# A hybrid decoder layer on one core: gates moved ahead of pooling, top-k rounds tile by tile, and small work taken off VectorE

## The chip, the cores and the metric

One Trainium2 chip, of which the kernel uses one core. The core has a matrix engine (TensorE, PE in the profile, with its weight loads as PEld), a vector engine (VectorE, DVE), a scalar engine (ScalarE, ACT), GpSimd (POOL) and SyncE (SP), which issues DMAs. Each engine runs its own queue in order and waits on semaphores. The metric is the device time of one execution in microseconds (us), the median of several runs.

## What is computed

One layer over x of 512 tokens by 1024 channels, in float32. One input projection feeds three token mixers; each mixer's output is gated, projected to 1024 channels, and the three are merged with sigmoid gates:

```python
u = x @ w_in + b_in                      # split into 19 pieces
y_a = pool_mixer(a_x) * silu(a_z)        # trailing means over 2, 4, 8, 16 tokens, per channel group
y_b = dsa_mixer(...) * silu(b_z)         # 8 heads, keys chosen per query: top 128 of an indexer's score
y_c = nsa_mixer(...) * silu(c_z)         # 8 heads in 2 groups: compressed, selected and window branches
g = sigmoid(g_merge).reshape(B, S, 3, D)
m = g[:,:,0] * (y_a @ w_pa) + g[:,:,1] * (y_b @ w_pb) + g[:,:,2] * (y_c @ w_pc)
return layernorm(alpha * x + m @ w_o)
```

The pooling mixer is `mean over the last w tokens - x`, where the first w-1 tokens divide by their position. The indexer's score is a sum over 8 heads of `relu(iq . ik) * iw`. The compressed branch has 31 blocks of 32 tokens, made by a small two-layer network.

## The kernel before

**Layout.** Activations lie with channels on the 128 partitions and the 512 tokens along the row. Each float32 operand is split into a rounded high part and a rest (`split`), and each product is three matmuls (`mm3`, lines L68 to L70). A "dense" tile is one 128-channel slice of the input projection: 8 slices of x times 3 matmuls of 128x512, 24 in all, written to a PSUM tile `d` (three buffers, shared with the pooling matmul). Its weights come by `load_w`: a DMA, the high part on ACT (L93), the rest on POOL (`w_l`, L95) in the middle of the program.

**Units.** Attention is done in units of four heads by 128 queries: for the third mixer ("c") two head groups g, token tiles j = 3, 2, 1, 0, and two branches each; then for the second mixer ("b") two groups with j = 0 to 3. A unit's front computes scores (`qkc`, `qkb`, L441, four PSUM buffers), masks them and takes the row maximum on DVE (L443), exponentiates on ACT (L448), scales (ACT L460, DVE L462 into `pc` or `pb`) and transposes by a DMA on SP; its back multiplies with the values (`acc`, L479) two half-units later. The compressed branch rides on the units of branch 0: class `Compressed` takes scores of 32 blocks, their least value after scaling by -0.125, softmax and gain (L505 to L521), and its matmuls are L529. The units of the first group end with a flag `"c0"`, those of the second with `"c1"`; later work that needs them waits in the list for the flag.

**Order.** The order of PE is written by hand. One list `F` of generators holds all other matmul work: dense tiles for queries, keys, SiLU gates (`f_zc`, `f_zb`), pooling (`pool_x`, `pool_z`, `pool_y`), merge gates (`merge_g`: a dense tile, then a tanh on ACT into `tg`) and merges (`merge`: projection `pp` of a mixer's output, times the gate). Between pieces of a unit the list is advanced by fixed steps (3.25 after each half front, 2 after a front, 0.3 per piece of the back). When the list stands at a flag that is not set, it gives nothing. The order on the other engines is set by a scheduler from the program.

**Top-k.** For token tiles 1, 2, 3 of the indexer the score `acc` (128 x 256, 384, 512) is turned into a mask by 16 rounds of `topk_round`: MAX8 (L305) finds the eight largest of each row, MATCH_REPLACE8 (L306) marks them. `tk(n)` issues n rounds from a list after each front, and the second mixer's unit j needs the mask of tile j.

**Pooling.** `pool_x` adds shifted rows on POOL (L566), and on DVE corrects the first columns through a small tile `pe` (L570, L571), forms mean minus x (L572), and copies the corrected columns back (L573). `pool_y` multiplies with 128x128 weights and reads the result on DVE (L588).

**Compressed values.** `compress_v` splits the block values into three bfloat16 parts and writes each into `VC` through a block mask (`bmask`, six multiplications, L396).

Of the kernel before, what the change touches and what calls it, by code (L numbers as in the profile page):

```python
# [7 lines left out]
F32 = mybir.dt.float32  # L8
# [4 lines left out]
OP = mybir.AluOpType  # L13
# [14 lines left out]
NTILES = I_G + 24  # L28
SMALL = (("posk", 32), ("posv", 32), ("pool_b", 4), ("pool_scale", 4), ("bmask", 4), ("rcnt", 16), ("rowv", 1),
         ("mcmp", 128), ("ident", 128))  # L30
# [4 lines left out]
def trunk(ctx, tc, a, out, dbg=None):  # L35
# [345 lines left out]
    def compress_v():  # L381
        HH, HL, w2h, w2l = CP["v"] + W2[1]
        bmask = small["bmask"]
        v32 = sp.tile([128, 2, 64], F32, name="vc32", bufs=1)
        ps = dps("vc")[:, :128].rearrange("p (g d) -> p g d", g=2)
        for g in range(2):
            mm3(ps[:, g], HH[:, g].rearrange("p r n -> p (r n)"), HL[:, g].rearrange("p r n -> p (r n)"),
                w2h, w2l, True, True)
        nc.vector.tensor_scalar(v32, ps, vscale, 0.5, op0=OP.mult, op1=OP.mult)
        for p in range(3):  # L390
            v1 = sp.tile([128, 2, 64], BF, name="vc1", bufs=2)
            nc.vector.tensor_copy(v1, v32)
            if p < 2:
                nc.vector.tensor_sub(v32, v32, v1)
            for g in range(2):
                nc.vector.tensor_mul(VC[p][:, g], v1[:, g, None, :].to_broadcast([128, 4, 64]),  # L396
                                     bmask[:, :, None].to_broadcast([128, 4, 64]))
        yield
# [85 lines left out]
    class Compressed:  # L484
# [5 lines left out]
        def begin(self, j, Q, K):  # L490
# [4 lines left out]
            if j == NT - 1:  # L495
# [12 lines left out]
        def probs(self):  # L508
            g, j, s = self.g, self.j, self.s
            den, r = sm("cden", 4, 2), sm("cr", 4, 2)  # L510
            nc.vector.tensor_sub(s, s, self.mx[:, :4, None].to_broadcast([128, 4, 32]))
            nc.scalar.activation(s, s, AF.Exp, scale=self.scale)
            nc.vector.tensor_reduce(den, s, AX.X, OP.add)
# [42 lines left out]
    def pool_x(g):  # L556
# [13 lines left out]
        nc.vector.tensor_mul(e[:, :w - 1], cur[:, :w - 1], PL["rcnt"][:, :w - 1])  # L570
        nc.vector.tensor_sub(e[:, :w - 1], e[:, :w - 1], x0[:, :w - 1])  # L571
        nc.vector.scalar_tensor_tensor(x0, cur, 1.0 / w, x0, op0=OP.mult, op1=OP.subtract)  # L572
        nc.vector.tensor_copy(x0[:, :w - 1], e[:, :w - 1])  # L573
        ph = PL["x", g] = big("t", "ph", F32R)
# [21 lines left out]

    def gate_d(d, br):
        i = I_G + 3 * d + br
        ps, b = yield from dense(i)
        t = big("b", "tg", F32, (128, 512))  # L600
        with tc.high_priority():
            nc.scalar.activation(t, ps, AF.Tanh, scale=0.5, bias=bhalf[:, i:i + 1])
        return t
# [14 lines left out]
    def merge_g(br, d):  # L618
        tg[br, d] = yield from gate_d(d, br)

    def merge(br, d):
        if d + 1 < KT:
            yield from merge_g(br, d + 1)
# [107 lines left out]
    F = Stream([(compress_in, I_KC, "k"), (vscales,), (compress_in, I_VC, "v"), (f_zc, 0, 0), (compress_mid, "k"),  # L731
                (f_zc, 0, 1), (compress_k,), (compress_mid, "v"), (f_qc, 1, 0), (f_qc, 1, 1), (f_pool,), (compress_v,),
                (pool_x, 0), (pool_x, 1), (pool_z, 0), (pool_z, 1), (f_kk, 1), (pool_y, 0), (f_zc, 1, 0), (pool_y, 1),
                (pool_x, 2), (pool_x, 3), (f_zc, 1, 1), (pool_z, 3), (pool_z, 2), (pool_y, 2), (f_qb, 0, 0), (pool_y, 3),
                (merge_g, 0, 0), "c0", (f_qb, 0, 1)] + [(merge, 0, d) for d in range(4)] +
               [(f_zb, 0, 0), (f_zb, 0, 1)] + [(merge, 0, d) for d in range(4, 7)] +
               [(merge_g, 2, 0), (merge, 0, 7), "c1", (f_qb, 1, 0), (f_qb, 1, 1), (f_zb, 1, 0), (f_zb, 1, 1)] +
               [(merge, 2, d) for d in range(KT)])
    ix = Stream([(index_scores, j) for j in (1, 2, 3)])
    while ix.step():  # L740
        F.step(2)
    rounds = [(topk_round, j) for _ in range(16) for j in (1, 2, 3)] + [(topk_end, j) for j in (1, 2, 3)]
# [44 lines left out]
    for w in work:  # L787
# [12 lines left out]
        else:  # L800
# [3 lines left out]
            if j:  # L804
                tk(100)
            un = Unit(f"b{g}{j}", psum_acc(), j, qb[g], KB[0], cmask[:, 384:] if j == 0 else negm[j],
                      0, None)
        for u in range(un.nsub):
            for _ in un.front(u):
                F.step(3.25)  # L810
            with tc.issue_after(un.last.ins):
                tk(2.3)
            nsub += 1
# [97 lines left out]
def layout(v):  # L911
# [70 lines left out]
```

## Time and profile before

| | us |
|---|---|
| runs (three) | 550.96, 550.22, 551.14; median 550.96 |
| profiled execution | 547.52 |
| its span, first to last instruction | 545.7 |
| TensorE busy in it | 519.2 |
| VectorE busy | 381.6 |
| ScalarE busy | 278.7 |
| GpSimd busy | 217.8 |

Busy time is the time in which an engine had an instruction in work; for PE it does not say at which clock. The profile also gives the granted TensorE clock (1.00 is full speed), and for each wait the engine and line that ended it. In tables of groups the form is: line, engine, operation, tile written and tiles read, shape and count, then busy us and mean ns of one.

### The profile page before, as it was taken

What the parts mean: (1) busy time and instruction counts of PE and PEld (TensorE: products, weight loads), DVE (VectorE), ACT (ScalarE), POOL (GpSimd) and SP (SyncE); (2) the same over time, 40 slices, a digit from 0 to 9 for tenths busy, and PEclk for the clock granted to TensorE, in tenths of its full rate; (3) what the DMA queues carried; (4) which work ended last, traced back from release to release, by engine and by line L of the source; (5) the groups of instructions that cost most, each with busy time, mean ns of one, the idle gap of its engine ahead of it and who ended that gap; (6) DMA issues with size and microseconds to landing.
All of it is one profiled execution on the core that took longest, in us unless ns stands there. A gap on an engine that the chain in (4) does not pass through costs nothing.

```text
span 545.7 us, 7778 instructions
## 1 busy us (share of the span) xinstructions
PE 519.2 (95%) x2718; PEld 420.2 (77%) x2718; DVE 381.6 (70%) x928; ACT 278.7 (51%) x561; POOL 217.8 (40%) x190
## 2 busy tenths in 40 slices
PE   7999989989999876999999999999999999999993
PEld 4899878868778654877778877787878888887883
DVE  5774898999999999888766466666441544545366
ACT  6783466655565475546566585765632333442000
POOL 0325433465557441134544355355564211316043
PEclk8999999989999997899999999999999999999997
DMA  7622331436545243365544445545553336454012
GB/s 271 261 77 78 115 117 59 121 79 154 95 114 126 64 116 82 84 165 129 154 102 114 123 130 132 126 117 127 139 140 96 117 111 207 164 185 144 1 60 94
DMA packets 82135, 66.72 MB, mean 122 GB/s; under 512 B 67184, under 2 KB 68656, under 8 KB 82096
## 3 DMA queue, kind: packets, MB, share of 16 engines
q1 hardware_dynamic: 74912, 40.54, 27.8%
q0 software_dynamic: 7184, 25.69, 15.4%
q8 instruction: 21, 0.34, 0.3%
q14 instruction: 18, 0.15, 0.1%
HBM read 47.87 MB, written 2.10 MB: 92 GB/s over the span
## 4 chain that ended last, share of the span: by engine, by line
PE 56%; DVE 9%; DMA 2%; ACT 1%; issue 1%; DVEq 0%; ACTq 0%
PE d L68 10%; PE d L70 10%; PE d L69 10%; PE pp L68 4%; PE pp L70 4%; PE pp L69 4%; PE acc L479 3%; PE wo L70 2%; PE wo L68 2%; PE wo L69 2%; PE qkb L441 2%; PE qkc L441 2%; DMA wo_st<-in_wo_dram 1%; DVE acc L306 1%; DVE m L305 1%
## 5 line engine op out<-in xcount | busy, mean ns | idle before, releaser
L68 PE MATMUL d<-xh,w_h 128*128 128x512 f32 (+1 forms) x424 | 168.6, 398 | 5.6 <-DVE za L588 2.8
L70 PE MATMUL d<-xh,w_l 128*128 128x512 f32 (+1 forms) x424 | 166.2, 392 | 0.0
L69 PE MATMUL d<-xl,w_h 128*128 128x512 f32 (+1 forms) x424 | 166.0, 392 | 0.0
L95 POOL TENSOR_TENSOR w_l<-w_st,w_h 128x1024 fp32r<-128x1024 f32 x41 | 99.8, 2436 | 130.1 <-ACT w_h L93 129.2
L68 PEld LDWEIGHTS d<-xh,w_h 128*128 128x128 f32 x424 | 80.5, 190 | 23.7 <-DVE za L588 3.3
L70 PEld LDWEIGHTS d<-xh,w_l 128*128 128x128 f32 x424 | 80.4, 190 | 17.5 <-DVE w_l L95 0.4
L69 PEld LDWEIGHTS d<-xl,w_h 128*128 128x128 f32 x424 | 80.5, 190 | 14.0
L93 ACT ACTIVATE w_h<-w_st 128x1024 fp32r<-128x1024 f32 x53 | 56.1, 1059 | 52.0 <-DMA w_st<-in_wt_dram 23.4
L448 ACT ACTIVATE qkc<-qkc,nb 128x512 f32<-128x512 f32 (+3 forms) x64 | 32.1, 502 | 44.3 <-DVE nb L443 28.6
L632 POOL TENSOR_TENSOR m<-m,tg 128x512 f32<-128x512 f32 x16 | 21.7, 1355 | 56.2 <-DVE tg L614 54.5
L95 POOL TENSOR_TENSOR wp_l<-wp_st,wp_h 128x512 fp32r<-128x512 f32 x16 | 20.5, 1281 | 53.9 <-ACT wp_h L93 53.9
L462 DVE SCALAR_TENSOR_TENSOR pc<-qkc,r,pc 128x512 f16<-128x512 f32 (+3 forms) x64 | 32.6, 543 | 8.6 <-ACT pc L460 8.3
L460 ACT ACTIVATE pc<-qkc,r 128x512 f16<-128x512 f32 (+3 forms) x64 | 29.6, 525 | 12.7 <-issue 5.5
L443 DVE CUSTOM_DVE_ANT_0 qkc<-qkc,cmask 128x512 f32<-128x512 f32 (+3 forms) x64 | 31.3, 490 | 4.4 <-PE qkc L441 4.0
L95 DVE TENSOR_TENSOR w_l<-w_st,w_h 128x1024 fp32r<-128x1024 f32 x12 | 15.6, 1306 | 19.4 <-ACT w_h L93 19.4
L448 ACT ACTIVATE qkb<-qkb,nb 128x128 f32<-128x128 f32 (+3 forms) x32 | 16.0, 500 | 23.3 <-DVE nb L443 23.0
L92 POOL DMA_DIRECT2D w_st<-in_wt_dram x41 | 23.3, 568 | 10.2 <-POOL w_l L95 6.8
L70 PE MATMUL wo<-woh,ml 128*128 128x512 f32 (+1 forms) x72 | 26.4, 367 | 0.3 <-DVE ml L65 0.3
L69 PE MATMUL wo<-wol,mh 128*128 128x512 f32 (+1 forms) x72 | 26.3, 366 | 0.0
L68 PE MATMUL wo<-woh,mh 128*128 128x512 f32 (+1 forms) x72 | 26.3, 365 | 0.0
L306 DVE MATCH_REPLACE8 acc<-m,acc 128x256 f32<-128x256 f32 (+2 forms) x48 | 25.7, 540 | 0.0
L479 PEld LDWEIGHTS <-vh 128*64 128x64 f16 x240 | 13.8, 110 | 15.1 <-issue 15.1
(245 smaller groups left out, 1031.7 us busy)
## 6 DMA issues: line engine op xcount, KB each, us to landing
w_st<-in_wt_dram POOLq DMA_DIRECT2D x41, 512.0 KB, 3.7
w_st<-in_wt_dram SPq DMA_DIRECT2D x12, 512.0 KB, 4.6
wp_st<-in_wp_dram POOLq DMA_DIRECT2D x16, 256.0 KB, 3.0
wo_st<-in_wo_dram SPq DMA_DIRECT2D x8, 512.0 KB, 3.5
xst<-in_xT_dram SPq DMA_DIRECT2D x8, 256.0 KB, 5.1
wp_st<-in_wp_dram SPq DMA_DIRECT2D x8, 256.0 KB, 2.6
z<-in_x_dram SPq DMA_DIRECT2D x4, 512.0 KB, 4.9
wvst<-in_wve_dram SPq DMA_DIRECT2D x4, 320.0 KB, 6.9
```

Of the source, the lines that this page charges most:

```text
L68: nc.tensor.matmul(ps, wh, rh, start=start, stop=False)
L69: nc.tensor.matmul(ps, wh, rl, start=False, stop=False)
L70: nc.tensor.matmul(ps, wl, rh, start=False, stop=stop)
L92: (nc.gpsimd if POOL[0] else nc.sync).dma_start(st, src)
L93: nc.scalar.activation(h[:, :n], st, AF.Copy)
L95: eng.tensor_sub(l[:, :n], st, f(h[:, :n]))
L306: nc.vector.match_replace(negm[j], m8, negm[j], MARK)
L443: nc.vector.tensor_tensor_reduce(sc[i], sc[i], self.mask, -0.125, 3e38, OP.add, OP.min, nb[:, i:i + 1])
L448: nc.scalar.activation(sc[i], sc[i], AF.Exp, scale=-1.0, bias=nb[:, i:i + 1], accum_out=den[:, i:i + 1])
L460: nc.scalar.activation(p[:, 0, i], sc[i], AF.Copy, scale=r[:, i:i + 1])
L462: self.last = nc.vector.scalar_tensor_tensor(p[:, 1, i], sc[i], r[:, i:i + 1], p[:, 0, i], op0=OP.mult, op1=OP.subtract)
L479: nc.tensor.matmul(self.acc[64 * i:64 * i + 64], v[:, k, self.vs * 64:self.vs * 64 + 64], pw[:, z, i, k], start=first, stop=False, skip_gr ...
```

## The change

1. Merge gates. `early_g` computes a gate into a larger tile `eg` that is kept until its merge. The gates of branch 0 for d = 0 to 3 stand ahead of pooling and between its parts; those of branch 2 for d = 0 to 3 ahead of `"c1"`. `merge` skips a gate that is there. The first query tile of the second mixer (`f_qb 0 0`) moves behind `"c0"`.
2. Top-k: the rounds of tiles 1 and 2 come first, in turns, with their ends, and then the 16 of tile 3; 1.7 rounds are issued after each front, not 2.3, and a unit of the second mixer takes only the rounds that it needs itself (`tk_until`).
3. Pooling: the corrected first columns are written in place and the main operation covers the others, so the copy L573 goes.
4. Compressed values: `VC` is cleared at the start by POOL, and POOL copies the four 32-partition blocks of each part (twelve copies); the mask and its columns in the `small` load go.
5. Compressed probabilities: the subtraction L511 goes; the least score is the bias of the exponential, one call for each head. For token tile 3 the maximum is first multiplied by -0.125.

```diff
-            for g in range(2):
-                nc.vector.tensor_mul(VC[p][:, g], v1[:, g, None, :].to_broadcast([128, 4, 64]),
-                                     bmask[:, :, None].to_broadcast([128, 4, 64]))
+            for h in range(4):
+                r = slice(32 * h, 32 * h + 32)
+                nc.gpsimd.tensor_copy(VC[p][r, :, h], v1[r])
...
-            nc.vector.tensor_sub(s, s, self.mx[:, :4, None].to_broadcast([128, 4, 32]))
-            nc.scalar.activation(s, s, AF.Exp, scale=self.scale)
+            for h in range(4):
+                nc.scalar.activation(s[:, h], s[:, h], AF.Exp, scale=self.scale, bias=self.mx[:, h:h + 1])
...
-        nc.vector.tensor_sub(e[:, :w - 1], e[:, :w - 1], x0[:, :w - 1])
-        nc.vector.scalar_tensor_tensor(x0, cur, 1.0 / w, x0, op0=OP.mult, op1=OP.subtract)
-        nc.vector.tensor_copy(x0[:, :w - 1], e[:, :w - 1])
+        nc.vector.tensor_sub(x0[:, :w - 1], e[:, :w - 1], x0[:, :w - 1])
+        nc.vector.scalar_tensor_tensor(x0[:, w - 1:], cur[:, w - 1:], 1.0 / w, x0[:, w - 1:], ...)
...
+    def early_g(br, d):
+        if d % 2 == 0:
+            EG[br] = big("s", f"eg{br}{d}", F32)
+        tg[br, d] = yield from gate_d(d, br, EG[br][:, d % 2])
...
-                (f_zc, 0, 1), (compress_k,), (compress_mid, "v"), (f_qc, 1, 0), (f_qc, 1, 1), (f_pool,), (compress_v,),
-                (pool_x, 0), (pool_x, 1), (pool_z, 0), (pool_z, 1), (f_kk, 1), (pool_y, 0), (f_zc, 1, 0), (pool_y, 1),
-                (pool_x, 2), (pool_x, 3), (f_zc, 1, 1), (pool_z, 3), (pool_z, 2), (pool_y, 2), (f_qb, 0, 0), (pool_y, 3),
-                (merge_g, 0, 0), "c0", (f_qb, 0, 1)] + [(merge, 0, d) for d in range(4)] +
-               [(f_zb, 0, 0), (f_zb, 0, 1)] + [(merge, 0, d) for d in range(4, 7)] +
-               [(merge_g, 2, 0), (merge, 0, 7), "c1", (f_qb, 1, 0), (f_qb, 1, 1), (f_zb, 1, 0), (f_zb, 1, 1)] +
-               [(merge, 2, d) for d in range(KT)])
+                (f_zc, 0, 1), (compress_k,), (compress_mid, "v"), (f_qc, 1, 0), (f_qc, 1, 1), (compress_v,),
+                (early_g, 0, 0), (f_kk, 1), (early_g, 0, 1), (f_pool,), (f_zc, 1, 0), (pool_x, 0), (early_g, 0, 2),
+                (pool_z, 0), (pool_x, 1), (early_g, 0, 3), (pool_y, 0), (pool_z, 1), (f_zc, 1, 1), (pool_x, 2), (pool_y, 1),
+                (pool_z, 2), (pool_x, 3), (pool_y, 2), (pool_z, 3), (pool_y, 3),
+                "c0", (f_qb, 0, 0), (f_qb, 0, 1)] + [(merge, 0, d) for d in range(3)] + [(f_zb, 0, 0), (f_zb, 0, 1)] +
+               [(merge, 0, d) for d in range(3, 7)] + [(early_g, 2, 0), (merge, 0, 7)] +
+               [(early_g, 2, d) for d in range(1, 4)] +
+               ["c1", (f_qb, 1, 0), (f_qb, 1, 1), (f_zb, 1, 0), (f_zb, 1, 1)] + [(merge, 2, d) for d in range(KT)])
...
-    rounds = [(topk_round, j) for _ in range(16) for j in (1, 2, 3)] + [(topk_end, j) for j in (1, 2, 3)]
+    rounds = [(topk_round, j) for _ in range(16) for j in (1, 2)] + [(topk_end, 1), (topk_end, 2)]
+    rounds += [(topk_round, 3)] * 16 + [(topk_end, 3)]
...
-                tk(2.3)
+                tk(1.7)
```

**PE, around the first unit of the second head group** (token tile 3, two heads; `acc2` is the back of the last units of the first group, `d26` and `d30` are dense tiles of pooling with weights `w26`, `w30`, `pool` is the pooling matmul). Before:

```order
L479 MATMUL acc2_152<-ptc000_2122,vh_140 64x256
L441 MATMUL qkc130_2321<-ks1_1517,cq11_1099 128x512 x2
L441 MATMUL qkc130_2326<-ks1_1517,cq11_1099 128x512 x2
L479 LDWEIGHTS vh_140
L479 MATMUL acc2_152<-ptc001_2217,vh_140 64x256
```

In the changed kernel:

```order
L480 MATMUL acc2_155<-ptc000_2060,vh_140 64x256
L442 MATMUL qkc130_2293<-ks1_1268,cq11_1100 128x512 x2
L68 MATMUL d26_2245<-xh3_87,w26_h_2240 128x512
L69 MATMUL d26_2245<-xl3_91,w26_h_2240 128x512
L70 MATMUL d26_2245<-xh3_87,w26_l_2241 128x512
L68 MATMUL pool_2322<-ph_2118,plhl_1363 128x512
L69 MATMUL pool_2322<-ph_2118,plhl_1363 128x512
L70 MATMUL pool_2322<-ph_2118,plhl_1363 128x512
L68 MATMUL d30_2338<-xh0_84,w30_h_2333 128x512
L69 MATMUL d30_2338<-xl0_88,w30_h_2333 128x512
L70 MATMUL d30_2338<-xh0_84,w30_l_2334 128x512
L442 MATMUL qkc130_2342<-ks1_1268,cq11_1100 128x512 x2
```

Where the list `F` stood at its flag, two score tiles followed each other; now dense and pooling matmuls lie between them, since two dense tiles more stand ahead of the flag than before (three gates in, one query tile out).

**DVE, in the second half-unit of the first head group** (`qkc` score tiles, `pc` their probabilities, `vc` compressed values, `acc_553`, `acc_690`, `acc_855` the scores of tiles 1, 2 and 3). Before:

```order
L443 ISA qkc_1226,nb<-qkc_1226,cmask 128x512
L443 ISA nb 128x1
L396 TENSOR_TENSOR vc_151<-vc_1128,small 128x256 x2
L462 SCALAR_TENSOR_TENSOR pc_1159<-qkc_1088,r,pc_1159 128x512
L462 SCALAR_TENSOR_TENSOR pc_1159<-qkc_1132,r,pc_1159 128x512
L305 MAX m_1178<-acc_855 128x8
L305 MAX m_1181<-acc_553 128x8
```

In the changed kernel (`acc_556` and `acc_693` are tiles 1 and 2):

```order
L463 SCALAR_TENSOR_TENSOR pc_1162<-qkc_1089,r,pc_1162 128x512
L393 CAST vc_1128<-vc_1105 128x128
L463 SCALAR_TENSOR_TENSOR pc_1162<-qkc_1134,r,pc_1162 128x512
L305 MAX m_1183<-acc_693 128x8
L305 MAX m_1186<-acc_556 128x8
L444 ISA qkc_1219,nb<-qkc_1219,cmask 128x512
```

The probabilities of the first half-unit stand ahead of the next score mask and no longer behind the mask multiplications, and tile 3 has left the top-k rows.

**POOL, at the same place** (`w_st` to `w_l` are weight loads and splits). Before:

```order
L92 DMA w_st<-in_wt_dram 128x1024
L95 TENSOR_TENSOR w_l<-w_st,w_h 128x1024
L566 TENSOR_TENSOR xs<-x_1203 128x511
L567 COPY xs<-x_1203 128x1
L92 DMA w_st<-in_wt_dram 128x1024
```

In the changed kernel:

```order
L95 TENSOR_TENSOR w_l<-w_st,w_h 128x1024
L398 COPY vc_149<-vc_1114 32x2x64 x4
L92 DMA w_st<-in_wt_dram 128x1024
L398 COPY vc_150<-vc_1121 32x2x64 x4
L398 COPY vc_151<-vc_1128 32x2x64 x4
L95 TENSOR_TENSOR w_l<-w_st,w_h 128x1024
```

The twelve copies stand where pooling's first shifted add stood, between two weight splits.

More of the change, by code (lines that the diff above doesn't have):

```diff
@@ L28 @@
 NTILES = I_G + 24
-SMALL = (("posk", 32), ("posv", 32), ("pool_b", 4), ("pool_scale", 4), ("bmask", 4), ("rcnt", 16), ("rowv", 1),
+SMALL = (("posk", 32), ("posv", 32), ("pool_b", 4), ("pool_scale", 4), ("rcnt", 16), ("rowv", 1),
          ("mcmp", 128), ("ident", 128))
@@ L315, in trunk @@
     VC = [cp.tile([128, 2, 4, 64], BF, name=f"vc{p}") for p in range(3)]
+    for p in range(3):
+        nc.gpsimd.memset(VC[p], 0.0)
     CP = {}
@@ L382, in compress_v @@
         HH, HL, w2h, w2l = CP["v"] + W2[1]
-        bmask = small["bmask"]
         v32 = sp.tile([128, 2, 64], F32, name="vc32", bufs=1)
@@ L502, in begin @@
                 nc.vector.tensor_reduce(self.mx[:, :4], self.s, AX.X, OP.max)
+                nc.vector.tensor_scalar(self.mx[:, :4], self.mx[:, :4], -0.125, None, op0=OP.mult)
         def score(self, h, ps):
@@ L570, in pool_x @@
         nc.vector.tensor_mul(e[:, :w - 1], cur[:, :w - 1], PL["rcnt"][:, :w - 1])
-        nc.vector.tensor_sub(e[:, :w - 1], e[:, :w - 1], x0[:, :w - 1])
-        nc.vector.scalar_tensor_tensor(x0, cur, 1.0 / w, x0, op0=OP.mult, op1=OP.subtract)
-        nc.vector.tensor_copy(x0[:, :w - 1], e[:, :w - 1])
+        nc.vector.tensor_sub(x0[:, :w - 1], e[:, :w - 1], x0[:, :w - 1])
+        nc.vector.scalar_tensor_tensor(x0[:, w - 1:], cur[:, w - 1:], 1.0 / w, x0[:, w - 1:], op0=OP.mult,
+                                       op1=OP.subtract)
         ph = PL["x", g] = big("t", "ph", F32R)
@@ L595, in trunk, with gate_d @@
     M32 = []
-    def gate_d(d, br):
+    def gate_d(d, br, t=None):
         i = I_G + 3 * d + br
         ps, b = yield from dense(i)
-        t = big("b", "tg", F32, (128, 512))
+        t = big("b", "tg", F32, (128, 512)) if t is None else t
         with tc.high_priority():
@@ L619, in merge_g @@
         tg[br, d] = yield from gate_d(d, br)
+    EG = {}
+    def early_g(br, d):
+        if d % 2 == 0:
+            EG[br] = big("s", f"eg{br}{d}", F32)
+        tg[br, d] = yield from gate_d(d, br, EG[br][:, d % 2])
     def merge(br, d):
-        if d + 1 < KT:
+        if d + 1 < KT and (br, d + 1) not in tg:
             yield from merge_g(br, d + 1)
@@ L750, in tk, with tk_until @@
             fn(j)
+    def tk_until(j):
+        while (topk_end, j) in rounds:
+            fn, i = rounds.pop(0)
+            fn(i)
     work = []
@@ L804, in trunk @@
             if j:
-                tk(100)
+                tk_until(j)
             un = Unit(f"b{g}{j}", psum_acc(), j, qb[g], KB[0], cmask[:, 384:] if j == 0 else negm[j],
@@ L961, in layout @@
     r["rowv"] = (t >= 31).astype(f4)[:, None]
-    r["bmask"] = (t[:, None] // 32 == np.arange(4)[None]).astype(f4)
     r["rcnt"] = c(np.broadcast_to((1.0 / np.arange(1, 17)).astype(f4), (128, 16)))
```

## The prediction

> **What bounds the kernel now.** I read the page's totals and clock line first, then each engine's busy time by stretches, then TensorE alone around the places where it stands still, then what it waited for there.
>
> ```profile
> PE   519.2 (95%) x2718; PEld 420.2 (77%) x2718; DVE 381.6 (70%) x928; ACT 278.7 (51%) x561; POOL 217.8 (40%) x190
> PEclk8999999989999997899999999999999999999997
> ```
>
> TensorE (PE) is busy 95% of the span, so only its pauses and the slices with a digit below 9 in the clock line can be won; the sum of its matmuls is not touched. The next rows are stretches of the span: length, then busy time of PE, PEld, DVE, ACT and POOL, then granted clock.
>
> ```profile
> 94.00:124.00 30.00, 27.54 (x116) 22.06 (x115) 27.88 (x69) 18.81 (x36) 15.54 (x13) 0.94 0.38 91
> 124.00:154.00 30.00, 30.00 (x176) 24.37 (x175) 29.58 (x77) 16.88 (x32) 15.71 (x14) 1.00 0.61 132
> 154.00:184.00 30.00, 30.00 (x174) 23.97 (x173) 28.53 (x83) 14.82 (x33) 17.71 (x21) 1.00 0.48 119
> 184.00:216.00 32.00, 22.84 (x119) 16.19 (x118) 30.57 (x98) 20.31 (x57) 12.07 (x10) 0.89 0.28 73
> 216.00:400.00 184.00, 182.02 (x993) 145.30 (x994) 127.16 (x383) 110.67 (x253) 83.16 (x65) 0.98 0.50 127
> ```
>
> From 94 to 216, the units of the first head group, DVE is busy 27.88 + 29.58 + 28.53 + 30.57 = 116.6 of 122 us: it is the bound there, and PE falls behind it at both ends. From 216 to 400 DVE has 184.0 - 127.2 = 56.8 us free. PE alone, cut where it stops and where its clock changes (length, PE busy, granted clock):
>
> ```profile
> 112.60:115.50 2.90, 0.43 (x3) 1.00 0.31 75
> 116.80:120.20 3.40, 3.40 (x10) 0.51 1.07 154
> 184.40:187.30 2.90, 0.35 (x3) 1.00 0.00 0
> 188.50:191.90 3.40, 3.40 (x12) 0.50 0.18 46
> 191.90:197.20 5.30, 4.98 (x35) 1.00 0.62 170
> 197.20:200.40 3.20, 0.38 (x2) 1.00 0.30 82
> 200.40:210.20 9.80, 9.30 (x58) 1.00 0.28 80
> 210.20:212.40 2.20, 0.52 (x6) 1.00 0.15 30
> 212.40:222.70 10.30, 7.04 (x27) 0.50 0.26 59
> ```
>
> Idle time (length less busy): 2.47 + 2.55 + 0.32 + 2.82 + 0.50 + 1.68 + 3.26 = 13.6 us. Half clock: 3.40 + 3.40 + 7.04 = 13.8 us of matmuls that took twice their time, so 6.9 us lost. Together **20.5 us**, all that this stage can give. What PE waited for:
>
> ```profile
> PE qkc L441 <- DVE pc L462: 5.5, 3, 2.7
> PE d L68 <- DVE za L588: 2.8, 1, 2.8
> PE d L68 <- ACT z L153: 2.6, 1, 2.6
> ```
>
> Score tiles wait until DVE has read the last ones (L462), projections until DVE has freed the PSUM of a pooling tile (L588). The ACT wait stands beside a pooling matmul too and ends when the DVE queue has moved on. All are DVE's queue.
>
> **The change part by part.** First what leaves DVE between 94 and 216 (rows: operation, shape, count, then busy us and mean ns):
>
> ```profile
> L305 DVE MAX8 m<-acc 128x8 f32<-128x512 f32 x9 | 6.1, 674 | 0.0
> L306 DVE MATCH_REPLACE8 acc<-m,acc 128x512 f32<-128x512 f32 x9 | 6.0, 671 | 0.0
> L305 DVE MAX8 m<-acc 128x8 f32<-128x384 f32 x10 | 5.4, 544 | 0.0
> L396 DVE TENSOR_TENSOR vc<-vc,small 128x256 bf16<-128x256 bf16 x6 | 5.3, 929 | 0.0
> L511 DVE TENSOR_TENSOR cs<-cs,cmx 128x128 f32<-128x128 f32 x5 | 4.9, 985 | 0.1
> L306 DVE MATCH_REPLACE8 acc<-m,acc 128x384 f32<-128x384 f32 x9 | 4.9, 540 | 0.0
> L305 DVE MAX8 m<-acc 128x8 f32<-128x256 f32 x10 | 4.1, 409 | 0.0
> L306 DVE MATCH_REPLACE8 acc<-m,acc 128x256 f32<-128x256 f32 x9 | 3.6, 405 | 0.0
> L573 DVE COPY x<-pe 128x15 f32<-128x15 f32 x1 | 2.3, 2334 | 0.0
> L573 DVE COPY x<-pe 128x3 f32<-128x3 f32 x1 | 2.0, 1962 | 0.0
> ```
>
> Top-k before: 9 x 674 + 10 x (544 + 409) + 9 x (671 + 540 + 405) ns = 30.1 us. After, the order puts 11 MAX8 and 10 MATCH_REPLACE of tiles 1 and 2 each ahead of the second head group and none of tile 3: 11 x (544 + 409) + 10 x (540 + 405) = 19.9 us. That is 10.2 us less. The six multiplications by the block mask: 5.3 us less. The small copies of pooling: 4.3 us less. The subtraction of the least compressed score: 4.9 us less; one 128x4 multiplication in its stead costs between nothing and the 0.3 us by which I shorten this, 4.6. Then two of the four pooling groups now stand behind the first unit of the second head group in DVE's order, with these five operations each:
>
> ```profile
> L572 DVE SCALAR_TENSOR_TENSOR x<-xs,x 128x512 f32<-128x512 f32 x4 | 4.9, 1236 | 0.1
> L407 DVE SCALAR_TENSOR_TENSOR za<-za,z 128x512 f32<-128x512 f32 x4 | 3.2, 788 | 0.0
> L65 DVE TENSOR_TENSOR yal<-za,yah 128x512 fp32r<-128x512 f32 x4 | 3.1, 768 | 0.0
> L65 DVE TENSOR_TENSOR ph<-x,ph 128x512 fp32r<-128x512 f32 x4 | 3.0, 761 | 0.0
> L588 DVE SCALAR_TENSOR_TENSOR za<-pool,small,za 128x512 f32<-128x512 f32 x4 | 2.9, 734 | 0.0
> ```
>
> 2 x (1236 + 788 + 768 + 761 + 734) = 8.6 us. Sum: 10.2 + 5.3 + 4.3 + 4.6 + 8.6 = 33.0, so DVE has 116.6 - 33.0 = 83.6 us to do there. PE's work in the same 122 us is its busy 27.54 + 30.00 + 30.00 + 22.84 = 110.4 less half of the half-clock pieces before 216 (3.4), about 107 us at full clock; its order has as many matmuls between the first units of the two head groups as before, only others. DVE thus falls from being the bound to 78% of PE's time. Between 124 and 184, at 97%, PE did not idle at all, so it is the pile-up that stops it, not the share.
>
> The gates also fill the hole at the end. Before, the stream of projections ran dry at its mark "c0", and the last acc matmuls of the group and the score tiles behind them stood bare; after, projections and pooling stand between them. The wait for the transposed probabilities is covered by that.
>
> What takes DVE's place: the top-k and the two pooling groups land after 216, 10.2 + 8.6 = 18.8 us against 56.8 free. The later work reaches no wait of PE there as long as that margin holds.
>
> POOL gets twelve 32x128 copies and three clears, and per moved gate a split and a DMA issue. ACT gets a tanh per gate, and four small exponentials for one:
>
> ```profile
> 109.47 2.39 POOL L95 TENSOR_TENSOR w_l<-w_st,w_h 128x1024 fp32r<-128x1024 f32 x1 [3.54 <-ACT w_h L93]
> 109.49 3.84 DVE L396 TENSOR_TENSOR vc<-vc,small 128x256 bf16<-128x256 bf16 x2
> L567 POOL COPY xs<-xs 128x8 f32<-128x8 f32 x1 | 0.2, 192 | 0.0
> L258 POOL CAST ki<-ki 64x512 fp32r<-64x512 f32 x1 | 0.6, 609 | 20.2 <-DVE ki L156 20.2
> L512 ACT ACTIVATE cs<-cs 128x128 f32<-128x128 f32 x5 | 1.6, 317 | 2.5 <-DVE cs L511 2.5
> L602 ACT ACTIVATE tg<-d,bhalf 128x512 f32<-128x512 f32 x1 | 0.7, 700 | 0.0
> ```
>
> A 32x128 copy lies between the 128x8 one and the 64x512 cast, 0.19 and 0.61 us; I take 0.25, near the small one, so 3 us for twelve (7.3 at worst). POOL is idle 30.0 - 15.5 = 14.5 us between 94 and 124, so either end is hidden. Behind the copies in POOL's queue stand a weight split and the two casts of the second group's keys. PE reaches that weight after three more projections, 72 matmuls or 12 us at the 176 in 30 us of the row from 124 to 154; if the copies held POOL longer than that, PE would wait by what is over. The three clears stand at the program's start, where POOL then waits 20.2 us for DVE (the ki row): nothing. Three gates more are 3 x 2.39 = 7.2 us of splits, while two pooling groups' shifted adds leave POOL: no net. Each DMA rides POOL's queue with its split, whose order is kept. SP's queue keeps its order. ACT: 3 x 0.70 for the gates and at most 3 x 0.317 for each of eight compressed units, 9.7 us in all, against 122 - 70.8 = 51 us free from 94 to 216 and 73 after.
>
> The first two rows above are why DVE's short operations cost so much: at 109.5 POOL starts a 2.39 us split, DVE a two-input operation, and two that could take 0.4 each take 3.84 us. The changed kernel has fewer such operations, but those left (splits, gains, sums) still meet POOL. For that I keep 0.32 + 0.50 us, the small pauses in the PE rows, and one more of 0.7, half the surplus of a mean stall: 1.5 us.
>
> A rule weighs against the part of the gain that is clock. The Trainium skill, "TensorE: Matmul & The Clock Gate", Part 1, says the clock falls to half after an idle window of about 3.4 us. By that rule stops of 2.5 to 3.2 us would not cause it, and removing them would return idle time alone. The rows say otherwise in three cases of four: half clock begins 1.3, 1.2 and 0 us after stops of 2.47, 2.55 and 1.68 us, and from 124 to 184, where PE never stops, the clock is 1.00 (the fourth stop, 2.82 us, is not followed by it). I take the rows.
>
> Sum: 20.5 - 1.5 = **19.0 us**. The profiled execution took 547.5 us (span 545.7), so 528.5; the median of the runs, 550.96, lies 3.4 higher, which I carry over: **532.0 us**.
>
> **The rivals.** (1) Clock stays: stops vanish, half clock does not. Gain 13.6 - 1.5 = 12.1, 538.9 us. For it, the one stop of four that half clock did not follow; against it, the other three. The Trainium skill's rule above would give this case. (2) Half is left: one of the two places, the start or the end of the stage, still stops, because the new hand-over between DVE and POOL (DVE's third cast waits for POOL's first copies, POOL's next copies for DVE) holds DVE's queue, or DVE and POOL keep meeting. The end is worth 2.55 + 0.32 + 2.82 + 0.50 + 1.68 + 3.26 + 5.2 = 16.3 us, the start 2.47 + 1.70 = 4.2; half of the end left gives about 540 us. For it: 3.84 us at 109.5; against it: 23 us of room. (3) Slower: top-k of tile 3 comes too late for the fourth unit of the second mixer. Its 16 rounds cost 16 x (674 + 671) = 21.5 us of DVE in one chain; if 15 or more were still to do when that unit's scores are ready, PE would stop for longer than is won, up to 553.5 us. The order speaks against it: one round alone stands between the third unit's last operations and that mask, and DVE keeps 56.8 - 18.8 = 38 us free from 216 to 400. (4) Nothing: the projections taken earlier are missed later, between the second group's units, and PE stops there instead, 551 us. Against it: DVE's 127.2 of 184 us there.
>
> **How the numbers follow.** Forecast 0.70, rival (1) 0.06, (2) 0.14, (3) 0.05, (4) 0.05. The range goes from 528, where all 20.5 us come and most of the 3.4 us between profiled execution and median does not, to 541, taking in (1) and (2). Faster by over 0.2% (1.1 us, about what a measurement of this kernel can tell): 0.70 + 0.06 + 0.14 = 0.90; (4) splits into 0.03 within and 0.02 slower; with (3) slower is 0.07.
>
> **What would show it.** Right: PE without a pause over 1 us from 94 to 231, its clock 1.00 throughout, DVE near 80% from 94 to 200 and busier than before from 216 to 400, the last MAX8 later than now, PE's waits on L462 and L588 gone. Wrong: a wait of PE on POOL's w_l after the copies, half-clock slices with no stop before them, or a wait of the second mixer's score tiles on the top-k.

## The result, and the profile of the changed kernel

The changed kernel takes 541.65 us (four runs, 541.23 to 542.48), the kernel before 550.59 on the same chip: ratio 0.984, 95% interval 0.982 to 0.986. It is faster by 8.9 us where 19.0 were forecast; the forecast was 532.0, and the time lies just above the range, which ended at 541. Its profiled execution took 541.9 us, with a span of 540.1.

The page's totals and clock line of the changed kernel:

```profile
PE 517.6 (96%) x2718; PEld 419.0 (78%) x2718; DVE 374.8 (69%) x912; ACT 283.1 (52%) x585; POOL 221.5 (41%) x205
PEclk9999999999999999799999899999999999999997
```

One deep slice is left in the middle, and there is a shallow new one further right. By stretches (length, busy time of PE, PEld, DVE, ACT, POOL, granted clock, then DMA share and GB/s):

```profile
94.00:124.00 30.00, 30.00 (x153) 24.50 (x153) 26.24 (x70) 21.49 (x42) 17.23 (x22) 1.00 0.51 115
124.00:154.00 30.00, 30.00 (x167) 24.21 (x166) 21.73 (x69) 19.35 (x42) 14.98 (x12) 1.00 0.55 146
154.00:184.00 30.00, 30.00 (x166) 24.38 (x166) 24.96 (x79) 16.33 (x43) 13.93 (x15) 1.00 0.42 103
184.00:216.00 32.00, 28.18 (x168) 21.74 (x166) 28.03 (x92) 21.68 (x59) 21.33 (x23) 1.00 0.40 105
216.00:231.00 15.00, 10.94 (x39) 8.63 (x40) 10.78 (x29) 6.39 (x12) 3.83 (x5) 0.77 0.34 78
216.00:400.00 184.00, 178.41 (x953) 141.08 (x954) 136.83 (x383) 107.99 (x253) 82.35 (x69) 0.97 0.48 120
```

The four old stops are gone: PE is busy throughout from 94 to 184. In their place stands one stop around 216, and from 216 to 400 PE now idles 5.6 us where it idled 2.0; 4.1 of these belong to that stop. The two waits of PE that are new, and PE alone at them (length, PE busy, clock):

```profile
PE pool L68 <- ACT ph L64: 7.5, 1, 7.5
PE pp L68 <- ACT tg L604: 1.5, 1, 1.5
```

```profile
212.50:220.00 7.50, 0.04 (x1) 0.81 0.56 134
217.20:224.00 6.80, 3.94 (x9) 0.50 0.31 70
300.50:302.00 1.50, 0.00 (x0) 1.00 0.08 30
302.50:305.90 3.40, 3.40 (x11) 0.51 0.80 159
```

The first stop costs 7.5 us, and 3.94 us of matmuls at half clock after it 2.0 more. The second costs 1.5 and 1.7. Where the kernel before lost 20.5 us between 94 and 231, this one loses 3.8 + 4.1 of idle time and 2.0 of half clock, 9.9 us; 3.2 us at 300 are new.

The long stop is the last pooling matmul (`pool_y 3`). The chain in front of it, from the timeline (start, length, engine, line; in brackets the idle time ahead and what ended it):

```profile
203.20 0.39 PE L70 MATMUL d<-xh,w_l 128*128 128x512 f32 x1
...
205.94 1.06 ACT L93 ACTIVATE w_h<-w_st 128x1024 fp32r<-128x1024 f32 x1
206.89 0.68 ACT L153 ACTIVATE x<-d,bias 128x512 f32<-128x512 f32 x1
...
207.09 2.39 POOL L95 TENSOR_TENSOR w_l<-w_st,w_h 128x1024 fp32r<-128x1024 f32 x1 [1.83 <-ACT w_h L93]
209.44 1.08 POOL L568 TENSOR_TENSOR xs<-x 128x511 f32<-128x511 f32 x1
...
214.60 1.27 POOL L95 TENSOR_TENSOR wp_l<-wp_st,wp_h 128x512 fp32r<-128x512 f32 x1 [0.92 <-ACT wp_h L93]
215.82 1.25 POOL L568 TENSOR_TENSOR xs<-xs 128x504 f32<-128x504 f32 x1
...
218.09 0.67 DVE L574 SCALAR_TENSOR_TENSOR x<-xs,x 128x497 f32<-128x497 f32 x1
...
219.38 0.63 ACT L64 ACTIVATE ph<-x 128x512 fp32r<-128x512 f32 x1 [1.33 <-DVE x L573]
...
220.06 0.79 PE L68 MATMUL pool<-ph,plhl 128*128 128x512 f32 x1 [7.52 <-ACT ph L64]
```

PE finishes the input tile of the fourth pooling group (`pool_x 3`) at 203.6. ACT reads it 3.3 us later, behind other work; POOL makes four shifted adds, with one weight split (2.39 us) in its queue ahead of the first and another (1.27 us) ahead of the last; then come DVE and ACT. From 203.6 to the pooling matmul at 220.1 that is 16.5 us. The new list leaves the gate tile of the same group between, 24 matmuls with pieces of a unit, which end at 212.5. In the old list the same pooling matmul had four dense tiles behind its input.

### The profile page after: what moved, and what is told of

It reads as the page before. It is cut to its first block, busy times and chain, and to the rows that moved or that the text cites. A ratio compares the mean times of both kernels' runs of the same rounds, so it can differ in the third digit from the quotient of the medians.

```text
span 540.1 us, 7802 instructions
## 1 busy us (share of the span) xinstructions
PE 517.6 (96%) x2718; PEld 419.0 (78%) x2718; DVE 374.8 (69%) x912; ACT 283.1 (52%) x585; POOL 221.5 (41%) x205
## 3 DMA queue, kind: packets, MB, share of 16 engines
q0 software_dynamic: 7184, 25.69, 15.6%
## 4 chain that ended last, share of the span: by engine, by line
PE 53%; DVE 11%; ACT 3%; DMA 2%; issue 1%; DVEq 0%; ACTq 0%
PE d L68 9%; PE d L70 9%; PE d L69 9%; PE pp L68 4%; PE pp L69 4%; PE pp L70 4%; PE acc L480 3%; PE wo L70 3%; PE wo L68 2%; PE wo L69 2%; PE qkb L442 2%; DVE pc L463 2%; DMA wo_st<-in_wo_dram 2%; PE qkc L442 2%; DVE acc L306 1%
## 5 line engine op out<-in xcount | busy, mean ns | idle before, releaser
L68 PE MATMUL d<-xh,w_h 128*128 128x512 f32 (+1 forms) x424 | 167.4, 395 | 0.2 <-DVE bk L333 0.2
L95 POOL TENSOR_TENSOR w_l<-w_st,w_h 128x1024 fp32r<-128x1024 f32 x41 | 98.2, 2396 | 125.6 <-ACT w_h L93 114.9
L463 DVE SCALAR_TENSOR_TENSOR pc<-qkc,r,pc 128x512 f16<-128x512 f32 (+3 forms) x64 | 32.8, 546 | 11.4 <-ACT pc L461 11.1
L642 POOL TENSOR_TENSOR m<-m,tg 128x512 f32<-128x512 f32 x12 | 16.6, 1380 | 53.4 <-DVE tg L616 53.2
L305 DVE MAX8 m<-acc 128x8 f32<-128x256 f32 (+2 forms) x48 | 25.4, 550 | 0.0
L95 DVE TENSOR_TENSOR w_l<-w_st,w_h 128x1024 fp32r<-128x1024 f32 x12 | 15.6, 1306 | 14.1 <-ACT w_h L93 14.1
L68 PE MATMUL pp<-yh,wp_h 128*128 128x512 f32 x64 | 25.3, 395 | 0.0
```

The source lines that it names most:

```text
L68: nc.tensor.matmul(ps, wh, rh, start=start, stop=False)
L95: eng.tensor_sub(l[:, :n], st, f(h[:, :n]))
L305: nc.vector.max(m8, negm[j])
L463: self.last = nc.vector.scalar_tensor_tensor(p[:, 1, i], sc[i], r[:, i:i + 1], p[:, 0, i], op0=OP.mult, op1=OP.subtract)
```

## The experiments

All ratios are to the kernel before on the same chip. My theory from these rows: the long stop is the **latency of a chain** that has too little cover. The rival: the queues of POOL and DVE are so full that the matmul waits wherever it stands.

**1 to 3. The input tile moved one or two dense tiles earlier, or next to its matmul** (the rest as in the changed kernel):

```diff
  changed: (f_zc,1,1),(pool_x,2),(pool_y,1),(pool_z,2),(pool_x,3),(pool_y,2),(pool_z,3),(pool_y,3)
+ one:     (f_zc,1,1),(pool_x,2),(pool_y,1),(pool_x,3),(pool_z,2),(pool_y,2),(pool_z,3),(pool_y,3)
+ two:     (pool_x,2),(pool_x,3),(pool_y,1),(f_zc,1,1),(pool_z,2),(pool_y,2),(pool_z,3),(pool_y,3)
+ next:    (f_zc,1,1),(pool_x,2),(pool_y,1),(pool_z,2),(pool_z,3),(pool_y,2),(pool_x,3),(pool_y,3)
```

> The fourth pooling group's input tile (pool_x 3) stands one dense tile earlier in the list, ahead of the third group's gate tile, so two dense tiles and not one lie between it and its pooling matmul (pool_y 3). Theory L (latency of the chain): the stop of 7.5 us at 212 in the changed kernel is the chain from that tile's end (206.4) to ACT's and DVE's halves of ph (220.0), 13.6 us, against 24 matmuls of cover; 24 more matmuls are 5.5 us, with the unit's pieces between them 6 to 7. The stop shrinks to 1 or 2 us, the half clock after it (3.4 us lost) may stay: 532 to 536 us. Rival H (hand-over: POOL's and DVE's queues are full there, with weight splits of 2.39 us and operations of DVE that POOL stretches, and the matmul would wait wherever it stands): the stop stays above 5 us, 539 us or more.

> The same tile stands still earlier, directly behind the third group's input tile, and three dense tiles lie between it and its pooling matmul (the gate tile f_zc 1 1 moves behind it). Theory L: 72 matmuls, 16 us and more, cover the 13.6 us chain, the stop and the half clock behind it are gone: 541.65 less 7.7 and less 3.4 is 530.5 us; 529.5 to 532. Rival H: the stop stays above 3 us or comes up at the third group's pooling matmul instead, whose adds share POOL's queue with the fourth's: 535 us or more.

> The other way: the fourth group's gate tile goes ahead of its input tile, and only the 3 matmuls of another pooling product lie between the input tile and its pooling matmul. Theory L: the cover falls by 24 matmuls, 5.5 us, and the stop grows by as much, to about 13 us; 546 to 548 us. Rival H: the chain is shorter when POOL has the gate's multiplication behind it already, and the stop stays at 7 to 9 us: 541 to 543.

Measured: one 0.994 (0.992 to 0.996), two 0.981 (0.978 to 0.984), next 0.991 (0.988 to 0.995). (The expectation put the tile's end at 206.4; the row above shows 203.6.) PE's longest waits in one, two and next, a fence each:

```profile
PE pool L68 <- ACT ph L64: 7.1, 2, 5.6
PE pool L69 <- DVE ph L65: 1.9, 2, 1.3
```

```profile
PE d L68 <- DVE za L590: 3.7, 1, 3.7
```

```profile
PE pool L68 <- ACT ph L64: 11.1, 1, 11.1
```

Neither theory had it whole. Taking the cover away makes the stop longer (11.1), as the latency theory says, and three tiles of cover remove it; but one tile more took only 2 us off the long stop, and opened a wait of 1.5 us at the third group's matmul. That kernel is even slower than the changed one, 0.994 against 0.984: its profile has a piece of 3.4 us at half clock behind the new wait, and another slow piece around 72, ahead of everything that the edit moved. The chain is not of fixed length. From ACT's read of the tile to its split `ph` it takes 8.0 us in next (213.81 to 221.77), 12.5 in the changed kernel and 22.5 in one. There POOL's last add stands behind a weight split that waits for ACT, and is through at 213.1; the other 8.3 us pass in DVE's queue, where the operations on the group's sums (L574 at 216.9, L573 at 221.2) stand behind a gate multiplication that waits for ACT, score masks, probabilities and top-k rounds. ACT's rows of the chain in next and in one:

```profile
213.81 0.69 ACT L153 ACTIVATE x<-d,bias 128x512 f32<-128x512 f32 x1
221.77 0.63 ACT L64 ACTIVATE ph<-x 128x512 fp32r<-128x512 f32 x1 [4.85 <-DVE x L573]
```

```profile
198.89 0.70 ACT L153 ACTIVATE x<-d,bias 128x512 f32<-128x512 f32 x1
...
221.35 0.63 ACT L64 ACTIVATE ph<-x 128x512 fp32r<-128x512 f32 x1 [2.88 <-DVE x L573]
```

In two, the wait passes to PSUM: a projection waits for the read of a pooling result (L590), which waits for its gate `za`.

**4. The stop filled with idle matmuls**, to price the clock:

```diff
         ps = dps("pool")
+        if g == 3:
+            for i in range(34):
+                nc.tensor.matmul(ps, PL["w"][:, 0, g], X(0, 0), start=True, stop=True)
```

> The changed kernel with 34 extra matmuls of 128x512 ahead of the last pooling matmul, into the same PSUM tile, which that matmul then overwrites; the list is as in the changed kernel. They are there to keep PE busy for the 7.7 us of the stop. Theory C (half clock follows the stop): no stop, the clock stays 1.00 from 205 to 235, the 3.4 us lost at half clock come back: 538.2 us, 537 to 539.5. Rival: the half clock has another cause there (the kind of work, or the time in the program): clock 0.5 for some 7 us as before, 541 to 542; or the extra matmuls delay what the chain waits for: 543 or more.

Measured: 538.67 us, 0.981 (0.978 to 0.983), which overlaps the changed kernel's interval. The clock line is plain:

```profile
PEclk9999989999999999999999999999999999999998
```

No half clock is left in the middle: it did follow the stop. Its price is the 2.0 us of the row above and not the 3.4 that I expected, because 2.8 of the slow piece's 6.8 us lay inside the stop. The time alone could not tell: in this profile the stop at 300, 1.5 us long here too, is not followed by half clock either.

**5. Both chains given distance** ("spread"; `...` is as in the changed kernel):

```diff
+ ...,(pool_z,1),(pool_x,2),(pool_y,1),(pool_x,3),(pool_z,2),(pool_z,3),(f_zc,1,1),(pool_y,2),
+ "c0",(f_qb,0,0),(pool_y,3),(f_qb,0,1),...
```

> The moves of pool_x alone gave 0.994 (one tile earlier) and 0.981 (two tiles) of the time before, and their traces showed the wait passing to the gate chain: in the second of them PE stopped 3.7 us for the read of a pooling result that waited for its gate za. Here both chains get distance: ahead of the third group's pooling matmul stand two dense tiles behind its gate tile, ahead of the fourth's three dense tiles behind its input tile and two behind its gate tile; the last pooling matmul stands behind the flag c0 and one query tile. Theory L (latency of the two chains against the dense tiles between): no stop of PE over 1 us and no half clock from 190 to 235; against the changed kernel's 0.984 that is 7.7 us of stop and 2 us of half clock, so 0.966, with 0.964 to 0.970 as its range (530 to 534 us where before takes 549 to 551). Rival H (POOL, DVE and ACT queues are so full there that some wait comes up wherever the matmuls stand): a stop of 2 us or more at another place, 0.975 to 0.985.

Measured: 0.974 (0.971 to 0.978), 534.8 us. The long stop is gone; three short ones are left, and the clock stays at 1.00 from 12 to 527:

```profile
PE d L68 <- DVE za L590: 2.2, 1, 2.2
PE pp L68 <- ACT tg L604: 1.5, 1, 1.5
PE pp L68 <- DVE bq L156: 1.5, 1, 1.5
```

**6 and 7. The change taken in two: all but the list, and the list alone** (6 in the changed kernel, 7 in the kernel before; the lists as in the diff of the change):

```diff
 6: -F = Stream([ new list ])
    +F = Stream([ old list, with merge_g ])
 7: -F = Stream([ old list ])
    +F = Stream([ new list ])
    +def early_g(br, d): ...
```

> The changed kernel with the list of before: no gate is taken early, all else of the change is in it (top-k by tile, the mask multiplications on POOL, pooling in place, the least score as bias). DVE loses 10.2 + 5.3 + 4.3 + 4.6 = 24.4 us between 94 and 216. Theory D (DVE's load made the four stops of before): the stops at 112 and at 184 to 200 shrink to under 1 us in all and their half clock goes; about 11 to 15 us won, 0.973 to 0.980. Rival F (the stops at the end come from the list that stands at its flag with nothing to give): those at 184 to 212 stay, only the first goes, 4 us won, 0.990 to 0.995.

> The kernel before with the new list and the early gates alone; top-k, mask multiplications, pooling's copies and the compressed subtraction as before. Theory D: DVE is relieved only by the two pooling groups that move out, 8.6 us, and stays the bound at 108 of 122 us; most of the 20.5 us stays, and the stop of the fourth group's chain (7.5 us, 2 us of half clock) comes on top: 1.00 to 1.015. Rival F: the list was what stood bare at the end; the end's 16 us go and the chain's 9.7 come: 0.985 to 0.990.

Measured: without the new list 0.986 (0.982 to 0.990), the list alone 0.985 (0.980 to 0.989), the two together 0.984: they do not add up. The stretch from 94 to 216 and the waits of the kernel without the new list:

```profile
94.00:216.00 122.00, 111.49 (x607) 88.68 (x606) 105.79 (x317) 77.60 (x184) 65.68 (x68) 0.97 0.44 111
```

```profile
PE qkc L442 <- DVE pc L463: 3.7, 3, 2.2
PE d L68 <- ACT z L153: 2.9, 1, 2.9
PE acc L480 <- DMA ptc<-pc: 2.1, 1, 2.1
```

and of the list alone:

```profile
94.00:216.00 122.00, 119.67 (x647) 95.66 (x645) 110.97 (x341) 74.13 (x165) 62.36 (x55) 0.99 0.52 116
```

```profile
PE pool L68 <- ACT ph L64: 7.5, 2, 6.1
```

With DVE down from 116.6 to 105.8 us but the old list, the stop at 112 goes and PE still idles 10.5 us at the end of the stage. With the new list and DVE still at 111.0, the old stops are gone, and the chain's is there. Experiment 7 lands in the range of its rival F; 6 lies between the ranges of its two theories.

The kernel without the new list shows one thing more. It has the top-k tile by tile, and PE does not idle in it from 231 to 400:

```profile
231.00:290.00 59.00, 59.00 (x327) 47.60 (x326) 43.55 (x144) 35.20 (x89) 27.29 (x21) 1.00 0.52 126
290.00:400.00 110.00, 110.00 (x603) 87.02 (x601) 78.48 (x204) 66.11 (x153) 53.52 (x45) 1.00 0.51 130
```

So the new order of the top-k alone does not make the stop at 300.

**8. The spread list alone, in the kernel before.** It differs from experiment 5 in one place also: `(pool_y,2)` stands ahead of `(f_zc,1,1)`, which experiment 9 tries in the changed kernel.

```diff
+ ...,(pool_z,1),(pool_x,2),(pool_y,1),(pool_x,3),(pool_z,2),(pool_z,3),(pool_y,2),(f_zc,1,1),
+ "c0",(f_qb,0,0),(pool_y,3),(f_qb,0,1),...
```

> The kernel before with the spread list and the early gates alone; none of the four parts that take work off DVE. Theory P (the place in the list, and not DVE's load, made the stops): no stop over 1.5 us from 94 to 231, within 0.005 of the kernel with all parts: 0.967 to 0.976. Rival D (load): DVE at 88 to 91% of the stage and its operations stretched by POOL bring stops back, 6 us or more: 0.980 to 0.990.

Measured: 0.972 (0.969 to 0.976), 534.2 us.

```profile
94.00:216.00 122.00, 122.00 (x673) 98.80 (x672) 110.95 (x336) 71.93 (x161) 63.68 (x57) 1.00 0.52 118
```

DVE is busy 111 of 122 us, and PE does not idle once, at full clock. All of DVE's old work is in the program; 5.6 us of it now fall outside this stretch. One wait comes at 219:

```profile
PE qkc L441 <- DVE pc L462: 2.5, 1, 2.5
```

It ends with L462 at 220.8, which stands in DVE's queue behind two splits (L65) and a score mask. The stops of 6 us or more that the rival asked for did not come.

**9 to 11. Place of one matmul, order and rate of the top-k** (9: the changed kernel with the list of 8; 10: with the old top-k too; 11: 9 with another rate):

```diff
10: -rounds = [(topk_round, j) for _ in range(16) for j in (1, 2)] + ...
    +rounds = [(topk_round, j) for _ in range(16) for j in (1, 2, 3)] + [(topk_end, j) for j in (1, 2, 3)]
    -tk_until(j)
    +tk(100)
10, 11: -tk(1.7)
        +tk(2.3)
```

> As the kernel with both chains spread (0.974), but the third group's pooling matmul stands ahead of the gate tile f_zc 1 1 and no longer behind it. In the trace of spread PE stopped 2.4 us at 219 because the read of that group's pooling result (L590) stood in DVE's queue behind the multiplication of that gate tile (L408, 220.35) although its own inputs were there at 215; DVE's order now has it ahead of the fourth group's L408. Theory Q (place in DVE's queue): that stop goes, 2.4 us or 0.0044: 0.970, range 0.967 to 0.972. Rival (the gate chain of the third group, with one dense tile between, is now too short): a stop of 1.5 us or more at the third group's pooling matmul or behind it: 0.973 or more.

> The kernel before this one with the top-k rounds as in the old kernel: all three tiles in turns, 2.3 rounds after each front, so that tile 3's rounds come early and none stands between 290 and 310. Theory T (the stop of 1.7 us at 295 to 302, which the kernels with the new list and the new top-k show and the one with the new list alone does not, comes from tile 3's rounds of 0.67 us in DVE's queue): the stop and any half clock behind it go, and the 10.2 us of DVE in the first stage cost nothing since the list covers them: 0.003 to 0.006 below the kernel without this edit. Rival D (DVE's load in the first stage does count): stops come back between 94 and 216, 0.005 or more above it.

> The kernel spread2 (0.981, where the one with the old top-k took 0.972) with 2.3 rounds of top-k after each front and not 1.7; the order by tile stays. Theory R (rate: tile 3's 16 rounds lie too late, up to 341, in the thick of the short units, where each holds a score mask for 0.67 us): they are through by about 290, the stops at 236 and 296 go: 0.970 to 0.974. Rival O (order: bunched tile by tile, three or four long operations of one kind stand ahead of a mask wherever they fall): a stop of 1.5 us or more comes up between 230 and 300 again: 0.977 or more.

Measured: 9: 0.981 (0.977 to 0.985); 10: 0.972 (0.969 to 0.975); 11: 0.984 (0.980 to 0.989). In 9 the aimed-at wait on L590 is gone, but its other waits, at 236 and 296, are those of 5 or longer, and half clock followed more of them; against 5 it decides nothing. 10 against 9 does: with the old top-k both of these waits go (one of 2.5 us at 219 comes), and the intervals do not overlap. The waits of 9, of 10 and of 11, a fence each:

```profile
PE pp L68 <- DVE bq L156: 2.5, 1, 2.5
PE pp L68 <- ACT tg L604: 1.5, 1, 1.5
```

```profile
PE qkc L442 <- DVE pc L463: 2.5, 1, 2.5
```

```profile
PE qkc L442 <- DVE pc L463: 2.9, 2, 1.7
PE pp L68 <- DVE bq L156: 2.8, 1, 2.8
```

A higher rate only moves the waits: the one at 296 goes, two at 202 and 221 come. So it is the order by tile with this list, and not the rate alone (10 also takes `tk_until` back, which no run separates from the order). Which of its operations stand in the way, no run separates either. Against 5, which has the top-k by tile and 0.974, the 0.972 of 10 is not separated.

**12. One exponential again** (in the changed kernel):

```diff
-nc.vector.tensor_scalar(self.mx[:, :4], self.mx[:, :4], -0.125, None, op0=OP.mult)
 ...
-for h in range(4):
-    nc.scalar.activation(s[:, h], s[:, h], AF.Exp, scale=self.scale, bias=self.mx[:, h:h + 1])
+nc.vector.tensor_sub(s, s, self.mx[:, :4, None].to_broadcast([128, 4, 32]))
+nc.scalar.activation(s, s, AF.Exp, scale=self.scale)
```

> The changed kernel with the compressed probabilities as before: the subtraction of the least score on DVE and one exponential for the four heads. Theory A: the four small exponentials, which wait one by one for DVE's maxima in ACT's queue, hold the weight split of ACT behind them, and make the stop of 1.5 us at 300 and its half clock (3.6 us lost in 300 to 310): those go, while DVE gets 4.9 us back between 94 and 216 where it has 20 us free, which costs nothing: 0.977 to 0.980. Rival T: the stop comes from DVE's rounds of the last top-k tile (0.68 us each) between the score masks there: stays, 0.984; and if DVE's 4.9 us count in the first stage, up to 0.992.

Measured: 0.988 (0.984 to 0.992), with the stop at 301 still there. The four small exponentials are not its cause. Against 0.984 the time is not separated.

**13 and 14. Two parts of the list, each alone in the kernel before:** pooling's order without early gates, and three early gates of branch 0 with pooling's old order. The early gates of branch 2 are in neither.

```diff
13: +...,(compress_v,),(f_kk,1),(f_pool,),(f_zc,1,0),(pool_x,0),(pool_z,0),(pool_x,1),(pool_y,0),(pool_z,1),(pool_x,2),
    +(pool_y,1),(pool_x,3),(pool_z,2),(pool_z,3),(pool_y,2),(f_zc,1,1),(f_qb,0,0),(pool_y,3),(merge_g,0,0),"c0",...
14: +...,(f_qc,1,1),(early_g,0,0),(early_g,0,1),(early_g,0,2),(f_pool,),(compress_v,),(pool_x,0),...
    -(pool_y,3),(merge_g,0,0),"c0",...
    +(pool_y,3),"c0",...
```

> The kernel before with pooling alone in the spread order (each pooling matmul one tile or more behind its gate tile and two or more behind its input tile), no gate taken early, f_qb 0 0 ahead of the last pooling matmul as before, all else as before. The list still runs dry at its flag. Theory P2 (pooling's distances made the stops at 184 and 197, the dry list those at 210 to 222): the first three stops go (2.6 + 2.7 + 3.0 us and 3.4 us of half clock), the two at 210 to 218 and their half clock stay: 11 us won, 0.978 to 0.982. Rival G (the early gates do it, by standing between the units): 0.990 or more.

> The kernel before with three gates of branch 0 taken early, ahead of pooling, and pooling itself in its old order and distances. Theory P2: the stops at 210 to 222 (2.9 + 2.6 us and 5 us of half clock) go since two more dense tiles stand ahead of the flag, and those of pooling (2.7 + 3.0 us, 1.7 us of half clock), now some 12 us later, stay: 10 us won and 7 left, 0.979 to 0.985. Rival G: all stops go, 0.970 to 0.975.

Measured: pooling's order 0.991 (0.987 to 0.994), the gates 0.979 (0.974 to 0.983). The stretch of each:

```profile
94.00:216.00 122.00, 112.25 (x609) 89.07 (x609) 116.11 (x345) 74.84 (x167) 61.87 (x56) 0.97 0.44 109
```

```profile
94.00:216.00 122.00, 119.45 (x655) 95.90 (x655) 110.24 (x340) 73.77 (x164) 64.69 (x58) 1.00 0.43 116
```

The gates carry most of it: they left 2.6 us of idle time in the stage where I expected pooling's 5.7. Pooling's order alone leaves 9.8, and the waits on `z` and `za` that it was to remove shrink from 2.6 and 2.8 us only to 1.4 each. But it takes the stop at 112 away with DVE as busy as before (27.78 of 30 us, 27.88 before):

```profile
94.00:124.00 30.00, 30.00 (x154) 24.50 (x154) 27.78 (x72) 19.64 (x38) 14.76 (x10) 1.00 0.42 101
```

Whether both parts are needed for 0.972 is not shown: the gates' interval, 0.974 to 0.983, overlaps that of 8, and their profile has a wait of 3.2 us at 318, in the second mixer, which 8 does not have.

## Why the prediction was wrong, step by step

- **"All are DVE's queue"** is the step that failed. DVE ended most of those waits, but its load did not make them. Experiment 8 has DVE at 91% and PE at 100%. Its DVE is 5.6 us below the kernel before in that stretch, so 6 and 14 are the sharper pair: DVE at 105.8 us leaves PE idle for 10.5 us, DVE at 110.2 for 2.6. Even the stop at 112 goes with the list alone, at the old load (13); in 6 it goes with the load under the old list, so either is enough there. The others came from what stood in the list: little or nothing between the last units once the list stood at its flag (14), and, in part, pooling matmuls close behind their inputs (13); how the two share it stays open. One of the waits was not ended by DVE at all, but by the DMA that transposes the probabilities (the row below, from the kernel before); it stays in 6 and 13 and goes with the early gates. I had seen that DVE at 97% between 124 and 184 stops nothing, and did not draw the conclusion.

```profile
PE acc L479 <- DMA ptc<-pc: 2.2, 1, 2.2
```

- **"The gates also fill the hole at the end ... projections and pooling stand between them"** was right for the old stops (14), and left out a term: the new list puts the last pooling matmul one tile behind its input, and a chain of 16.5 us had 9 us of cover. Idle 7.5 and half clock 2.0, 9.5 us in all, none of it in the sum. The case "half is left" came near in its time, 540 us, but by this mechanism and not by the hand-over of the copies: that is luck.
- **33.0 us off DVE** was mis-sized: DVE fell from 116.6 to 101.0 from 94 to 216, by 15.6. Part of this is that the kernel runs ahead and does work in the stretch that stood behind 216 before: three groups of pooling and not two, 13 and 12 MAX8 rounds of tiles 1 and 2 and not 11, 12 of the 512-wide L463 and not 8. And DVE's operations were still stretched beside POOL's: of the four L574, the one at 167.4, under a weight split of POOL, took 2.69 us, the one at 218.1 0.67. The prediction's reading that the order has "as many matmuls between the first units of the two head groups as before" was wrong too, since two dense tiles more stand ahead of the flag.
- **"The later work reaches no wait of PE there"** failed: at 300 a wait of 1.5 us with 1.7 us of half clock. It is gone with the new list and the old top-k (7 and 10), and with the new top-k and the old list (6); 14, with three early gates and the old top-k, keeps 1.1 us of it.
- **The 3.4 us carried over** from profile to median were not there: the profile of the changed kernel took 541.9, its median 541.65. The missing 13.4 us between the forecast profile, 528.5, and the measured one are 9.9 - 1.5 in the stage and 3.2 at 300; the other 1.8 were not traced one by one.
- **Right:** the stops at 112, 184, 197 and 210 and the waits on L462 and L588 went; the clock was 1.00 from 94 until the new stop. The twelve copies took 0.29 us each, and PE waited for no weight split. Top-k of tile 3 came in time for its unit.
- **What the change's parts are worth:** the list in its better order gives all of the 0.972. The mask on POOL, pooling in place and the biased exponentials add nothing that shows (10 against 8), and the top-k by tile costs with the list of 8 (9 against 10); with the list of 5 no cost is shown. Experiments 8 and 10, at 0.972 both, beat both kernels.

## What to carry to other kernels

A wait that ends when a busy engine answers is not yet proof that this engine's load is the cause: ask first how much work stands between the producer and the consumer in the waiting engine's own order, and how long the chain between them is. When a list is rewritten, price each pair of producer and consumer anew, with every queue that the chain crosses. A chain over several engines has no fixed length: 8 to 22 us here from ACT's read to ACT's split, by what the other queues put ahead of its links.

## What the runs showed of the hardware that I had not expected

A stop of 1.5 us can be followed by half clock or not, in the same place of nearly the same program. At 296, in experiment 5 and then in experiment 9 (PE: the stop, then the piece behind it):

```profile
294.90:296.70 1.80, 0.25 (x4) 1.00 0.22 87
297.00:301.00 4.00, 4.00 (x21) 1.00 0.80 191
```

```profile
296.20:297.90 1.70, 0.17 (x2) 1.00 0.22 87
299.10:302.50 3.40, 3.40 (x12) 0.50 0.84 221
```

Shorter stops can do it too. Around 72 every kernel has a stop that no experiment aims at. In the changed kernel it is 1.5 us long and the clock stays at 1.00; in experiment 9 it is 1.2 us long, and this follows:

```profile
73.80:80.60 6.80, 6.80 (x33) 0.50 0.22 78
```

The slow pieces come in lengths of about 3.4, 6.8 and 10.2 us (the longest in the kernel before, from 212.4 on). So the price of a stop is not fixed; the runs of experiment 9, one program, went from 534.4 us at a mean clock of 0.997 to 541.0 at 0.983. The Trainium skill, "TensorE: Matmul & The Clock Gate", Part 1, has a free-running window of about 3.4 us, which agrees with these lengths and with the chance; its condition of an idle window of that length does not, since stops of 1.2 and 1.5 us were enough here.
